# The first norm's sum of squares cut into two fp32r halves and summed by two products at blocks 38 and 39

## The chip, the cores and the metric

One NeuronCore of a Trainium2 chip runs the whole program. The metric is the device time of one execution in microseconds (us); lower is better. The engines named here: TensorE (PE, with its weight loads as PEld), VectorE (DVE), ScalarE (ACT), GpSimd (POOL) and SyncE (SP, which issues nearly all transfers).

## What is computed

One inference step of a two-layer decoder for 256 prompt tokens and 8 sample tokens that share all weights: 264 columns in all (`T = 264`), with a model width of 1024. Each layer is a mixer (layer 0: block-sparse attention beside a gated MLP; layer 1: stick-breaking attention beside a pooling mixer) and a feed-forward part with a short convolution. All parts begin with a root-mean-square norm. The part that the change touches is the very first norm and the projection behind it:

```python
def rmsnorm(x, g):
    xf = x.astype(jnp.float32)
    y = xf * lax.rsqrt(jnp.mean(xf * xf, axis=-1, keepdims=True) + EPS)
    return (y * g).astype(x.dtype)
...
    h = rmsnorm(x, norm_g)
    z = h @ w_in
    q, k, v, bu, bv = jnp.split(z, [...], axis=-1)
```

All arrays are float32.

## The kernel before

Activations lie transposed: the model width is on the 128 partitions in 8 tiles of 128x264, the tokens along the free axis. A matrix product is cut into blocks of 128x128 weights against one 128x264 tile. Each float32 operand is written as a high and a low part in the format fp32r (`wh`, `wl` for weights, `xg_h`, `xg_l` for activations), and each block is three products on TensorE: high by high, high by low, low by high. The layer-0 input projection has 20 output tiles of 8 blocks each, 160 blocks; one output tile of PSUM collects 8 blocks.

The high part of the weights is made by ScalarE (a copy that rounds), the low part by VectorE (the difference), for a weight tile of 8 blocks at a time: weight tile t holds blocks 8t to 8t+7. In the loop of blocks (`run`), `split(t)` makes the parts up to three tiles ahead, on lines L321. For the first tiles the order is written out by hand ahead of the loop: `part`, `operand`, `square` and `whole(tt)` (L734 for the high part, L735 for the low part). Four slots hold weight parts, so tile 7 takes the place of tile 3, which is free when block 31 is through. Tile 5 comes from a transfer of its own; tiles 6 and 7 come from one transfer of 1 MB, which is issued at 9.64 us.

The norm's factor R is needed only after the projection, since it scales columns. So the squares of the eight input tiles are made on ScalarE (`square`, L713), summed to one 128x264 tile by three additions on VectorE (`add`, L759), and summed over partitions by a product with a matrix of ones into the PSUM tile `ns_n0`. ScalarE turns that into R with a logarithm and an exponential (L502, L503). Then VectorE scales the output tiles that have collected by then (`in0_evac`, L807 for bv), which frees their PSUM banks, and makes the scaled rotary tables (L775). Blocks 0 to 31 are the output tiles bv0 to bv3 in four banks; blocks 32 to 39 (q0) and 40 to 47 (q1) go to two spare banks of another pool; block 48 needs the bank of bv0 again.

The program is traced in Python in the order of the code. A planner then puts each engine's instructions in order, by its own idea at build time of when each is ready: an instruction whose inputs come early may go ahead of one that was traced before it. `tc.keep_in_program_order(i)` pins an instruction behind the one that was traced just before it on the same engine. An engine issues its instructions strictly in the order so set, and waits where an input is missing. In this stage all instructions of TensorE are pinned (`fixed[0] = True`), and so are those of `whole`, `square`, `operand` and `add`; those of `split` are not. Hooks are functions called between blocks: `blk(38, f)` calls `f` after block 37 and ahead of block 38. `norm0` is hooked there in the kernel before: the float32 product, the logarithm and exponential, then the pinned evacuations.

Of the kernel before, what the change touches and what calls it, by code (L numbers as in the profile page):

```python
# [9 lines left out]
F32 = mybir.dt.float32  # L10
# [4 lines left out]
ALU = mybir.AluOpType  # L15
# [4 lines left out]
D = 1024  # L20
# [3 lines left out]
T = SEQ + NS  # L24
# [190 lines left out]
def tile_decoder_step(ctx: ExitStack, tc: tile.TileContext, a):  # L215
    nc = tc.nc
    v, s, g = nc.vector, nc.scalar, nc.gpsimd
# [14 lines left out]
    pe = TensorE()  # L232
# [10 lines left out]
    def f4(name, shape=(P, 4, T), dt=F32):  # L243
        return up.tile(list(shape), dt, tag="u", name=name)
# [7 lines left out]
    def at(name):  # L252
        return psa.tile([P, 512], F32, tag="at", name=name)
# [14 lines left out]
    def vec(n):  # L268
        o, w = _VEC[n]
        return VEC[:, o:o + w]  # L270
# [24 lines left out]
    def wtiles(tt):  # L295
        return [wsp.tile([P, 8 * P], F32R, tag=f"w{x}", name=f"w{x}{tt}") for x in "hl"]
# [97 lines left out]
    first, o = [], 0  # L394
# [34 lines left out]
    onesr = con.tile([P, P], F32R, name="onesr")  # L429
# [13 lines left out]
    class Norm:  # L443
# [8 lines left out]
        def add(self, m, src=None):  # L452
            q = sm.tile([P, T], F32, tag="sq", name=f"sq_{self.name}{m}")
            i = s.activation(q, X[:, m, :] if src is None else src, AF.Square)
            if src is not None:
                tc.keep_in_program_order(i)
            if m == KD - 1 and self.two:
                self.last.append(q)
            elif self.acc is None:
                self.acc = q  # L460
            elif m == (0 if self.seeded else 1):
                n = sm.tile([P, T], F32, tag="acc", name=f"acc_{self.name}", bufs=2)
                g.tensor_tensor(n, self.acc, q, ALU.add)
                self.acc = n
            else:
                g.tensor_tensor(self.acc, self.acc, q, ALU.add)

        def finish(self, pin=False, cut=False, inv=False):
            if not cut:
                return rstd_of([self.acc] + self.last, 1.0 / D, self.name, pin, eps=not self.seeded)  # L470
            return rstd_of(cut_sum(self.acc, self.name), 1.0 / D, self.name, pin, w=onesr, inv=inv)

    cast = [None]

    def cut_sum(x, name):
        if name in ("f0", "n1", "f1"):
            h, l = [pp.tile([P, 384], F32R, tag="p", name=f"acc{c}_{name}")[:, o:o + T] for c, o in (("h", 24), ("l", 16))]
        else:
            h, l = [sm.tile([P, T], F32R, tag="rz", name=f"acc{c}_{name}", bufs=4) for c in "hl"]
        cast[0] = s.activation(h, x, AF.Copy)  # L480
        g.tensor_tensor(l, x, h.bitcast(F32), ALU.subtract)
        return [h, l]

    def rstd_of(parts, scale, name, pin=False, bank=None, w=None, inv=False, eps=True):
        p = (bank or at)(f"ns_{name}")
        for i, x in enumerate(parts):
            mm = pe.matmul(p[:, :T], ones if w is None else w, x, start=i == 0, stop=i == len(parts) - 1)
            if pin:
                tc.keep_in_program_order(mm)
        R = sm.tile([P, T], F32, tag="R", name=f"R_{name}", bufs=2)  # L490
        if inv:
            L = sm.tile([P, T], F32, tag="rinv", name=f"L_{name}", bufs=1)
            s.activation(L, p[:, :T], AF.Ln, bias=epst, scale=scale)
            s.activation(R, L, AF.Exp, scale=-0.5)
            last[0] = s.activation(L, L, AF.Exp, scale=0.5)
            return R, L
        return rstd_from(p, scale, name, eps, R)

    def rstd_from(p, scale, name, eps=True, R=None):
        if R is None:  # L500
            R = sm.tile([P, T], F32, tag="R", name=f"R_{name}", bufs=2)
        s.activation(R, p[:, :T], AF.Ln, bias=epst if eps else 0.0, scale=scale)  # L502
        last[0] = s.activation(R, R, AF.Exp, scale=-0.5)  # L503
        return R
# [175 lines left out]
    def residual(gain, name, operand=True, R=None, plain=False):  # L680
        xg = [mv(f"xg_{name}{i}") for i in range(2)] if operand else None
        nrm = Norm(name, not operand)

        def evac(m, o):
            m = m[1]
            if R is not None and not plain:
                z = sm.tile([P, T], F32, tag="rz", name=f"z_{name}{m}", bufs=4)
                v.tensor_tensor(z, o, R, ALU.mult)
                o = z
            if plain and m == KD - 1:  # L690
                end(o)
                return
            v.tensor_tensor(X[:, m, :], X[:, m, :], o, ALU.add)
            if operand:
                operand_tile(xg[m // 4], m, X[:, m, :], gain[:, m:m + 1])
            nrm.add(m)
            if not operand:
                s.activation(X[:, m, :], X[:, m, :], AF.Copy, scale=gain[:, m:m + 1])
        return xg, nrm, evac
# [9 lines left out]
    nrm = Norm("n0")  # L709
    sqw = [f4(f"sqw{i}") for i in range(2)]  # L710
# [15 lines left out]
    def whole(tt, cut=(0, 8)):  # L726
        if tt not in splits:
            splits[tt] = wtiles(tt)
        c = slice(cut[0] * P, cut[1] * P)
        h, l = [x[:, c] for x in splits[tt]]  # L730
        ci = chunk_of[tt]
        o = (tt * 8 - coff[ci]) * P
        src = raws[ci][:, o + c.start:o + c.stop]
        tc.keep_in_program_order(s.activation(h, src, AF.Copy))  # L734
        tc.keep_in_program_order(v.tensor_tensor(l, src, h.bitcast(F32), ALU.subtract))  # L735
# [24 lines left out]
    add(sqw[0], sqw[0], sqw[1])  # L760
    add(sqw[0][:, 0:2, :], sqw[0][:, 0:2, :], sqw[0][:, 2:4, :])
    add(sqw[0][:, 0, :], sqw[0][:, 0, :], sqw[0][:, 1, :])
    whole(5)
    nrm.acc = sqw[0][:, 0, :]
    whole(6)
    rope = f4("rope")
    R0, held = [], []

    def norm0():
        R = nrm.finish(pin=True)  # L770
        R0.append(R)
        for m, o in held:
            tc.keep_in_program_order(in0_evac(m, o))
        for i in range(2):
            tc.keep_in_program_order(v.tensor_tensor(rope[:, i, :], CS[:, i, :], R, ALU.mult))  # L775

    maskb0 = con.tile([P, 384], BF16, name="maskb0")
    g.memset(maskb0[:, P:SEQ], 0.0)
# [9 lines left out]
    def in0_evac(m, o):  # L788
        n, t = m
        if not R0:  # L790
            held.append((m, o))
            return
        if n in "qk":
            d = (q4 if n == "q" else k4)[:, t, :]
            z = sm.tile([P, T], F32, tag="rz", name=f"rz_{n}{t}", bufs=4)
            v.stream_shuffle(z, o, shuf)
            if n == "q":
                v.scalar_tensor_tensor(d, o, SCALE, rope[:, 0, :], ALU.mult, ALU.mult)
            else:
                v.tensor_tensor(d, o, rope[:, 0, :], ALU.mult)  # L800
            if n == "q":
                v.scalar_tensor_tensor(z, z, SCALE, rope[:, 1, :], ALU.mult, ALU.mult)
            else:
                v.tensor_tensor(z, z, rope[:, 1, :], ALU.mult)
            v.tensor_tensor(d, d, z, ALU.add)
        else:
            return v.tensor_tensor({"v": v4, "bv": bv4, "bu": bu4}[n][:, t, :], o, R0[0], ALU.mult)  # L807
# [116 lines left out]
    def gm_mean():  # L924
        st0["acc"] = cut_sum(sum4(SUM1, bv4, "bsum"), "bsum")

    def gm_var():
        pmu = mmb("pmu")
        for i, x in enumerate(st0["acc"]):
            pe.matmul(pmu[:, :T], onesr, x, start=i == 0, stop=i == 1)  # L930
        mu = sm.tile([P, T], F32, tag="sq", name="mu")
        i = s.activation(mu, pmu[:, :T], AF.Copy, scale=1.0 / 512)
        behind(st0["exp", 5, 0], i)
        behind(st0["exp", 5, 1], i)
        ahead[18] = i, v.tensor_tensor(bv4, bv4, mu.unsqueeze(1).to_broadcast([P, 4, T]), ALU.subtract)
        sq4 = f4("sq4")
        s.activation(sq4, bv4, AF.Square)
        st0["acc"] = cut_sum(sum4(SUM2, sq4, "bsq"), "bsq")
# [36 lines left out]
    blk = lambda b, f, *x: hk.at(b / 8 - 1, f, *x)  # L975
# [12 lines left out]
        blk(92 + 6 * n, drip_of(vload, 2))  # L988
    for m in range(0, KD, 2):
        blk(120 + 4 * m, late_x, m)  # L990
    blk(38, norm0)
    blk(40, masks)
    blk(44, gm_first)
    blk(72, sm_q)
# [35 lines left out]
    xg, nrm, evac = residual(vec("f0"), "f0")  # L1030
    run(orders["out0"], pick([catA, catB]), evac, hk)
    fixed[0] = False
    R = nrm.finish(cut=True)
# [177 lines left out]
    blk = lambda b, f, *x: hk.at(b / 8 - 1, f, *x)  # L1211
# [31 lines left out]
    xg, nrm, evac = residual(vec("f1"), "f1")  # L1243
    run(orders["out1"], pick([catA, catB]), evac, hk)
    fixed[0] = False
    R, RI = nrm.finish(cut=True, inv=True)
    gelu_set()
    _, nrm, evac = residual(vec("fin"), "fin", operand=False, R=R, plain=True)
# [37 lines left out]
    o = P * KD * TF  # L1286
# [81 lines left out]
```

## Time and profile before

| what | value |
|---|---|
| median of 3 runs | 588.69 us (588.42 to 589.29) |
| the profiled execution's own time | 588.17 us |
| its span in the trace | 586.4 us |
| granted TensorE clock | 0.999 |
| PE busy | 579.3 us, 99% of the span |
| DVE busy | 433.4 us, 74% |
| ACT busy | 340.1 us, 58% |
| POOL busy | 47.7 us, 8% |

All times of instructions in this document are from the start of the span. A row of the timeline gives the start, the length, the engine, the source line, the operation, and output<-inputs by the program's names without their numbers (so `ns_n` is `ns_n0`, and `mm` any of the accumulating tiles); equal neighbours are merged with their count (x2), and what stands in brackets is how long the engine was idle before and what ended it. The ends of PE's rows are modelled, since matmuls overlap; its rate is read from the starts.

### The profile page before, as it was taken

How to read it: one execution, taken by the hardware profiler on the slowest of the kernel's cores; microseconds unless marked ns; L12 is line 12 of the kernel's file. 1: busy time of each engine (PE TensorE's matmuls, PEld its weight loads, DVE VectorE, ACT ScalarE, POOL GpSimd, SP SyncE). 2: the span in 40 equal slices, each digit the busy share in tenths (PEclk: the TensorE clock that was granted, in tenths of full speed). 3: DMA queues.
4: the chain of work that ended last, by engine and by line, in shares of the span. 5: the costliest groups of instructions: out<-in, count | busy, mean ns of one | idle time of the engine just before them, and what ended most of it. 6: DMA issues, size and time to landing. Idle time of an engine off the chain costs nothing.

```text
span 586.4 us, 12433 instructions
## 1 busy us (share of the span) xinstructions
PE 579.3 (99%) x4976; PEld 564.5 (96%) x4976; DVE 433.4 (74%) x778; ACT 340.1 (58%) x603; POOL 47.7 (8%) x62
## 2 busy tenths in 40 slices
PE   9999999999999999999999999999999999999995
PEld 8999979999999999999999879999999999999995
DVE  6999976787877878656669867777787777865561
ACT  7849746665655656544454557567565565664431
POOL 1001313200000000011030000120000000011011
PEclk9999999999999999999999999999999999999999
DMA  8999564554545455984557853555454546454502
GB/s 326 414 354 412 205 222 181 174 211 154 207 154 206 164 197 172 343 321 177 200 210 269 307 201 99 181 191 180 181 193 167 203 158 216 157 211 154 208 1 74
DMA packets 28140, 122.42 MB, mean 209 GB/s; under 512 B 3378, under 2 KB 5298, under 8 KB 16690
## 3 DMA queue, kind: packets, MB, share of 16 engines
q1 hardware_dynamic: 27792, 121.30, 57.6%
q8 instruction: 39, 0.64, 0.4%
q10 hardware_dynamic: 290, 0.32, 0.2%
q14 instruction: 19, 0.16, 0.1%
HBM read 117.65 MB, written 3.96 MB: 207 GB/s over the span
## 4 chain that ended last, share of the span: by engine, by line
PE 99%; DVE 0%; ACT 0%; DVEq 0%; issue 0%
PE mm L227 92%; PE sc L227 1%; PE pv_l L227 1%; PE pav L227 1%; PE warm L227 1%; PE pt L230 1%; PE Z L227 1%; PE S L227 1%; PE pf L227 0%; DVE yo L1294 0%; PE pm L227 0%; PE vtp_v L230 0%; PE ns_end L227 0%; PE ns_n L227 0%; PE po_l L230 0%; PE vtp_sgu L230 0%
## 5 line engine op out<-in xcount | busy, mean ns | idle before, releaser
L321 ACT ACTIVATE wh<-raw 128x1024 fp32r<-128x1024 f32 x177 | 187.5, 1060 | 195.2 <-PE mm L227 187.6
L321 DVE TENSOR_TENSOR wl<-raw,wh 128x1024 fp32r<-128x1024 f32 x177 | 216.9, 1226 | 107.9 <-ACT wh L321 106.9
L227 PE MATMUL mm<-xg_f_h,wh 128*128 128x264 f32 x704 | 199.9, 284 | 0.0
L227 PE MATMUL mm<-xg_f_h,wl 128*128 128x264 f32 x704 | 199.8, 284 | 0.0
L227 PE MATMUL mm<-xg_f_l,wh 128*128 128x264 f32 x704 | 198.6, 282 | 0.0
L227 PEld LDWEIGHTS mm<-xg_f_l,wh 128*128 128x128 f32 x704 | 132.8, 189 | 0.0
L227 PEld LDWEIGHTS mm<-xg_f_h,wh 128*128 128x128 f32 x704 | 132.5, 188 | 0.0
L227 PEld LDWEIGHTS mm<-xg_f_h,wl 128*128 128x128 f32 x704 | 132.4, 188 | 0.0
L227 PE MATMUL mm<-a_h,wh 128*128 128x264 f32 x352 | 100.0, 284 | 0.0
L227 PE MATMUL mm<-a_h,wl 128*128 128x264 f32 x352 | 99.9, 284 | 0.0
L227 PE MATMUL mm<-a_l,wh 128*128 128x264 f32 x352 | 99.3, 282 | 0.0
L227 PEld LDWEIGHTS mm<-a_l,wh 128*128 128x128 f32 x352 | 66.4, 189 | 0.0
L227 PEld LDWEIGHTS mm<-a_h,wh 128*128 128x128 f32 x352 | 66.2, 188 | 0.0
L227 PEld LDWEIGHTS mm<-a_h,wl 128*128 128x128 f32 x352 | 66.2, 188 | 0.0
L227 PE MATMUL mm<-xg_h,wh 128*128 128x264 f32 x160 | 42.9, 293 | 0.0
L227 PE MATMUL mm<-xg_h,wl 128*128 128x264 f32 x160 | 41.7, 284 | 0.0
L227 PE MATMUL mm<-xg_l,wh 128*128 128x264 f32 x160 | 41.5, 284 | 0.0
L227 PE MATMUL mm<-xg_n_h,wh 128*128 128x264 f32 x128 | 36.8, 287 | 0.0
L227 PE MATMUL mm<-xg_n_h,wl 128*128 128x264 f32 x128 | 36.3, 284 | 0.0
L227 PE MATMUL mm<-xg_n_l,wh 128*128 128x264 f32 x128 | 36.2, 283 | 0.0
L227 PEld LDWEIGHTS mm<-xg_h,wh 128*128 128x128 f32 x160 | 28.6, 189 | 1.8 <-issue 1.2
L227 PEld LDWEIGHTS mm<-xg_l,wh 128*128 128x128 f32 x160 | 28.6, 189 | 0.0
(264 smaller groups left out, 852.2 us busy)
## 6 DMA issues: line engine op xcount, KB each, us to landing
raw<-in_w SPq DMA_DIRECT2D x89, 1024.0 KB, 4.8
K<-in_kt SPq DMA_DIRECT2D x32, 256.0 KB, 5.4
V<-in_vp SPq DMA_DIRECT2D x32, 256.0 KB, 5.5
raw<-in_w SPq DMA_DIRECT2D x3, 512.0 KB, 7.1
xw<-in_xw SPq DMA_DIRECT2D x3, 388.0 KB, 4.8
X<-in_x SPq DMA_DIRECT2D x4, 264.0 KB, 5.7
out_y<-yo SPq DMA_DIRECT2D x3, 184.0 KB, 2.3
out_k<-k SPq DMA_DIRECT2D x1, 528.0 KB, 7.5
```

The source lines that it names most:

```text
L227: return self.keep(nc.tensor.matmul(*x, **k))
L230: return self.keep(nc.tensor.transpose(*x, **k))
L321: for i, j in zip((s.activation(h, src, AF.Copy), v.tensor_tensor(l, src, h.bitcast(F32), ALU.subtract)), ahead.pop(tt, ())):
```

## The change

The sum of squares is no longer multiplied as float32. `cut_sum` gets a form for it (`pin=True`): ScalarE copies the sum to a high half in fp32r, pinned where it is traced, between the last `square` and the high part of weight tile 5; VectorE makes the low half, pinned where it is traced, between the low parts of weight tiles 5 and 6. The product with ones becomes two fp32r products into `ns_n0`: the high half's ahead of block 38, the low half's ahead of block 39. The logarithm, the exponential and the evacuations move from the hook at 38 to the one at 39, behind the second product. The PSUM tile is claimed ahead of the loop and no longer at block 38.

```diff
-    def cut_sum(x, name):
+    def cut_sum(x, name, pin=False):
...
             h, l = [sm.tile([P, T], F32R, tag="rz", name=f"acc{c}_{name}", bufs=4) for c in "hl"]
         cast[0] = s.activation(h, x, AF.Copy)
+        if pin:
+            tc.keep_in_program_order(cast[0])
+            return [h, l], lambda: tc.keep_in_program_order(v.tensor_tensor(l, x, h.bitcast(F32), ALU.subtract))
         g.tensor_tensor(l, x, h.bitcast(F32), ALU.subtract)
         return [h, l]
...
     add(sqw[0][:, 0, :], sqw[0][:, 0, :], sqw[0][:, 1, :])
+    x0, low0 = cut_sum(sqw[0][:, 0, :], "n0", pin=True)
     whole(5)
-    nrm.acc = sqw[0][:, 0, :]
+    low0()
     whole(6)
...
     def norm0():
-        R = nrm.finish(pin=True)
+        p = at("ns_n0")
+
+        def one(i):
+            tc.keep_in_program_order(pe.matmul(p[:, :T], onesr, x0[i], start=i == 0, stop=i == 1))
+
+        blk(38, one, 0)
+        blk(39, one, 1)
+        blk(39, lambda: root0(p))
+
+    def root0(p):
+        R = rstd_from(p, 1.0 / D, "n0")
         R0.append(R)
-        for m, o in held:
+        for m, o in held[:4]:
             tc.keep_in_program_order(in0_evac(m, o))
         for i in range(2):
             tc.keep_in_program_order(v.tensor_tensor(rope[:, i, :], CS[:, i, :], R, ALU.mult))
+        for m, o in held[4:]:
+            in0_evac(m, o)
...
-    blk(38, norm0)
+    norm0()
```

## Prediction

> **What bounds the kernel now.** I read the page's table of engines first, then the chain of waits in order of time for the first 60 us, then the timeline of each engine from 12 to 24 us, where the change lies.
>
> ```profile
> PE 579.3 (99%) x4976; PEld 564.5 (96%) x4976; DVE 433.4 (74%) x778; ACT 340.1 (58%) x603; POOL 47.7 (8%) x62
> 4.78 14.14 PE mm L227 x114
> 18.92 0.45 PE ns_n L227 x2
> 19.36 21.15 PE mm L227 x174
> PEld mm L227 <- issue: 2.8, 6, 0.8
> ```
>
> TensorE is busy for 99% of the span, and the chain runs through it alone: 114 products (38 blocks), the sum for the norm, then 174 more. The last row, of the view of waits, is the largest stop ahead of ordinary weight loads: 2.8 us in the whole span. So a product saved on TensorE is time saved, and a wait put into TensorE's stream is time lost, for little downstream could give it back.
>
> ```profile
> 18.51 0.28 PE L227 MATMUL mm<-xg_l,wh 128*128 128x264 f32 x1
> 18.64 0.28 PE L227 MATMUL mm<-xg_h,wl 128*128 128x264 f32 x1
> 18.76 0.61 PE L227 MATMUL ns_n<-sqw,ones 128*128 128x264 f32 x2
> 19.01 0.48 PE L227 MATMUL mm<-xg_h,wh 128*128 128x264 f32 x1
> 19.32 0.28 PE L227 MATMUL mm<-xg_l,wh 128*128 128x264 f32 x1
> 19.44 0.28 PE L227 MATMUL mm<-xg_h,wl 128*128 128x264 f32 x1
> 19.57 0.29 PE L227 MATMUL mm<-xg_h,wh 128*128 128x264 f32 x1
> 22.74 0.28 PE L227 MATMUL mm<-xg_h,wl 128*128 128x264 f32 x1
> 22.86 0.34 PE L227 MATMUL mm<-xg_h,wh 128*128 128x264 f32 x1
> 23.04 0.28 PE L227 MATMUL mm<-xg_l,wh 128*128 128x264 f32 x1
> ```
>
> Ordinary products start every 0.12 us. The float32 sum comes at 18.76; block 38 really begins 0.12 before its second product, at 19.20, and block 39 at 19.57. So the sum costs 0.44 us (the chain says 0.45). At 22.86, block 48, one step is 0.18 instead of 0.12: the bank of bv0 comes free a touch late.
>
> ```profile
> 14.06 1.35 ACT L713 ACTIVATE sqw<-xw 128x264 f32<-128x264 f32 x4
> 15.32 1.05 ACT L734 ACTIVATE wh<-raw 128x1024 fp32r<-128x1024 f32 x1
> 18.61 1.06 ACT L734 ACTIVATE wh<-raw 128x1024 fp32r<-128x1024 f32 x1 [2.25 <-DMA raw<-in_w]
> 19.57 1.05 ACT L321 ACTIVATE wh<-raw 128x1024 fp32r<-128x1024 f32 x1
> 20.52 0.46 ACT L502 ACTIVATE R_n<-ns_n,epst 128x264 f32<-128x264 f32 x1
> 21.02 0.43 ACT L503 ACTIVATE R_n<-R_n 128x264 f32<-128x264 f32 x1
> 15.51 1.25 DVE L759 TENSOR_TENSOR sqw<-sqw,sqw 128x1056 f32<-128x1056 f32 x1
> 16.80 1.18 DVE L759 TENSOR_TENSOR sqw<-sqw 128x528 f32<-128x528 f32 x2
> 17.89 1.22 DVE L735 TENSOR_TENSOR wl<-raw,wh 128x1024 fp32r<-128x1024 f32 x1
> 19.70 1.23 DVE L735 TENSOR_TENSOR wl<-raw,wh 128x1024 fp32r<-128x1024 f32 x1 [0.59 <-ACT wh L734]
> 20.84 1.22 DVE L321 TENSOR_TENSOR wl<-raw,wh 128x1024 fp32r<-128x1024 f32 x1
> 21.99 0.46 DVE L796 STREAM_SHUFFLE rz_q<-mm 128x264 f32<-128x264 f32 x1
> 22.34 1.43 DVE L807 TENSOR_TENSOR bv<-mm,R_n 128x264 f32<-128x264 f32 x4
> ```
>
> This is the stretch that decides. On ScalarE the high part of weight tile 5 (15.32) goes ahead while VectorE still adds the squares; the additions end at 16.80 + 1.18 = 17.98. Then ScalarE waits for the transfer of tiles 6 and 7, which lands at 18.61. All this lay hidden: TensorE needs tile 5 only at block 40, 8 x 3 x 0.12 us ahead of block 48 (22.86), at about 19.93.
>
> **The change, part by part.** *TensorE.* Two fp32r products at 0.12 each replace 0.44: -0.20 us. By itself TensorE would reach the first at 18.76, block 38 at 18.88, the second at 19.24 and block 39 at 19.36.
>
> *ScalarE: the new cast of the high half.* It is pinned between the last square and tile 5. Its input is the third addition, so ScalarE, which issues in order, stands from 15.41 until 17.98, and what was done at 15.32 comes behind it: tile 5's high part, then tile 6's.
>
> *VectorE: the low half.* It is pinned behind tile 5's low part, which waits for tile 5's high part, which waits for the cast. And TensorE's second product waits for the low half ahead of block 39. So the wait is a chain: additions, cast, high 5, low 5, low half, product, and behind the product all of TensorE.
>
> ```profile
> 35.56 0.43 DVE L805 TENSOR_TENSOR q<-q,rz_q 128x264 f32<-128x264 f32 x1
> 36.08 0.27 ACT L977 ACTIVATE qz_l<-q 64x32 f32<-64x32 f32 x1 [0.40 <-DVE q L805]
> 4.06 0.52 ACT L437 ACTIVATE xg_h<-xw 128x264 fp32r<-128x264 f32 x1 [1.02 <-DMA xw<-in_xw]
> 4.63 0.65 PEld L227 LDWEIGHTS mm<-xg_h,wh 128*128 128x128 f32 x4 [0.33 <-ACT xg_h L437]
> ```
>
> Its links: a hand-over from VectorE to ScalarE takes 0.09 (35.99 to 36.08), one to TensorE 0.05 (taken from 4.58 to 4.63). ScalarE goes on 0.31 after starting a 128x264 tile (four squares: (1.35 - 0.41)/3) and 0.96 after a weight tile (18.61 to 19.57). VectorE starts a low part 1.09 after ScalarE starts the high part (18.61 to 19.70), goes on 1.14 later (19.70 to 20.84), and needs 0.43 for a 128x264 difference. The cast isn't in the trace; the square of the same shape bounds it below (0.41), the scaled copy above (0.52).
>
> *What the planner does with ScalarE's hole.* The high part of tile 7 (19.57, L321) isn't pinned. Its slot is free when block 31 is through: 18 + 1 products ahead of 18.76, about 16.6, well before the additions end. The trace shows that the planner fills such holes: the shuffle of q0 (21.99) was traced behind the four pinned bv evacuations (22.34) and runs ahead of them, because they wait for R. That this shuffle goes first also says that in the plan low 7 was through before R was, so the plan had tile 7 landed early. The chip has it land at 18.61. So I expect tile 7's high part in the hole ahead of the cast, where it holds the cast until the transfer lands. The two ends are then:
>
> - hole unfilled: cast 17.98 + 0.09 = 18.07, high 5 at 18.38, low 5 at 19.47, low half 20.61 to 21.04, product at 21.09. TensorE waits 21.09 - 19.24 = 1.85, block 39 begins at 21.21 instead of 19.57: +1.64.
> - hole filled by tile 7: high 7 at 18.61, cast 19.57, high 5 at 19.88, low 5 at 20.97, low half 22.11 to 22.54, product at 22.59. Block 39 begins at 22.71: +3.14. TensorE waits twice, at the first product (cast ready at 19.57 + 0.41 + 0.05 = 20.03, so 1.27) and at the second (20.52 to 22.59: 2.07).
>
> I take the second end, because tile 7 is ready some 1.4 us before the additions end, and keep both for the range.
>
> *Behind it.* Block 40 comes 0.36 after block 39 (23.07), with tile 5's low part ready since 22.2: no new wait. R comes at 22.59 + 0.28 + 0.05, then from 20.52 to 21.44 it takes 0.92: 23.84; bv0 is out by about 24.6, and block 48 comes at 26.0. So the 0.06 at 22.86 goes: -0.06. VectorE's queue after tiles 6 and 7 is some 1.7 us later than before and TensorE over 3, so later evacuations and low parts gain slack. The moved hook carries no transfer; SP's queue keeps its order, and the pool slot of the squares, held about 3 us longer, can delay one tile load at most as long as TensorE is late itself. GpSimd gets nothing. The earlier claim of the PSUM tile and `held[4:]` (empty, since q0 ends with block 39) cost nothing.
>
> *Sum:* 3.14 - 0.06 = +3.08 us, in which the -0.20 is contained. Against the profiled execution's 588.17 (span 586.4 and 1.8 around it) 591.25. That execution lies 0.52 under the median of 588.69, so for a median I say 588.69 + 3.08 = 591.8.
>
> **The rivals.** *Hole unfilled* (tile 7 stays behind tile 6, as in the order of before). For it: tracing order, and that the plan's transfer of tile 7 may be later than the additions. +1.64 - 0.06 = +1.58: 590.3.
>
> *The clock halves.*
>
> ```profile
> 0.78 4.00 PE L227 MATMUL warm<-const-bfloat16-1.0 128*128 128x256 bf16 x18 [0.78 <-PEq L1334]
> ```
>
> The first 18 products take 4.00/18 = 0.22 each, those after 4.63 only 0.12: TensorE starts at about half rate for some 3.6 us. If a wait of 2 us set it back, some 3.6 us at half rate would lose 1.8 more: 593.6. Against it: two separate waits, each shorter than that stretch; for it: the trace has no idle stretch of that size to show either way.
>
> The Trainium skill, "TensorE: Matmul & The Clock Gate", Part 1, says the clock drops to half after at least one idle window of about 3.4 us and comes back after as long a busy one. By that rule neither wait fills a window and nothing is added. No run here shows such a gap yet.
>
> *Not slower: tile 5 keeps its place ahead of the cast.* If ScalarE ran high 5 at 15.32 as now and only the cast waited, low 5 would stay at 17.89, the low half would follow at 19.03 (17.89 + 1.14) and end at 19.46, and the product start at 19.51: a wait of 0.27 against the 0.20 saved and the 0.06, zero in sum: 588.7. What decides is whether the high part of tile 5 starts before 18.0. Against it: the pin puts it behind the cast, and ScalarE's rows are in order throughout.
>
> **How the numbers follow.** A difference of 0.2% (1.18 us) is about what a measurement here can tell. Hole filled 0.48; hole unfilled 0.32; clock 0.06; tile 5 ahead 0.09; something else that the new plan does 0.05. Filled and clock are slower by over 0.2%, of unfilled (0.27%) I give 0.28 to slower and 0.04 to within; tile 5 ahead is within; of the rest 0.03 goes to faster and 0.02 to within. Slower 0.82, within 0.15, faster 0.03. The range holds both ends with 0.4 below the unfilled case (late waits that give a little back) and 0.6 above the filled one (a slower cast, a hand-over): 589.9 to 592.4, with 0.8 inside.
>
> **What would show it.** Right: on ScalarE an fp32r copy of the sum standing ahead of tile 5's high part (L734), with idle time before it; tile 7's high part (L321) ahead of both; a VectorE difference of 128x264 behind tile 5's low part, ending near 22.5; two `ns_n` products 2 to 2.6 us apart, with PE idle before them; no 0.18 step at block 48; 0.12 us steps throughout. Wrong: high 5 at 15.3; the two products 0.5 us apart with no idle; a step of 0.22 after the gap (clock); or a wait of similar size taken away elsewhere.

## The result, and the profile after

| what | before | after |
|---|---|---|
| median | 588.66 us (588.42 to 589.29, 6 runs) | 593.48 us (592.65 to 594.13, 6 runs) |
| profiled execution | 588.17 us | 593.34 us |

The change makes the kernel 4.8 us slower: ratio 1.0082, interval 1.0072 to 1.0092. The forecast of 591.8 had the direction; the time lies 1.1 above its range. Three stops of TensorE, not one, make most of the difference. First the page's table of engines, then three rows of the view of waits (us waited in all, times, longest), after; the last row is the kernel before, for the transposes:

```profile
PE 580.8 (98%) x4976; PEld 565.3 (96%) x4976; DVE 434.0 (73%) x779; ACT 343.4 (58%) x606; POOL 46.9 (8%) x62
PEld mm L227 <- DVE bv L823: 2.0, 1, 2.0
PEld ns_n L227 <- DVE accl_n L483: 1.8, 1, 1.8
PEld pt L230 <- DVE st L848: 0.6, 1, 0.6
...
PEld pt L230 <- DVE st L832: 0.2, 1, 0.2
```

ScalarE has three instructions more, though the change adds one to it. TensorE's longest single wait is not the one for the low half (`accl_n`) but one for `bv`, the evacuation that needs R. The third is at the first transposes of the attention (`pt`), where before the row had 0.2. The lines moved by up to 16: L737 and L738 are the parts that were L734 and L735, L505 and L506 the logarithm and exponential, L823 the evacuation.

TensorE's timeline after:

```profile
19.87 0.28 PE L227 MATMUL ns_n<-acch_n,onesr 128*128 128x264 f32 x1
20.24 0.28 PE L227 MATMUL mm<-xg_h,wl 128*128 128x264 f32 x1
22.15 0.39 PE L227 MATMUL ns_n<-accl_n,onesr 128*128 128x264 f32 x1 [1.63 <-DVE accl_n L483]
22.38 0.29 PE L227 MATMUL mm<-xg_h,wh 128*128 128x264 f32 x1
25.53 0.28 PE L227 MATMUL mm<-xg_h,wl 128*128 128x264 f32 x1
27.56 0.39 PE L227 MATMUL mm<-xg_h,wh 128*128 128x264 f32 x1 [1.74 <-DVE bv L823]
27.78 0.28 PE L227 MATMUL mm<-xg_l,wh 128*128 128x264 f32 x1
27.90 0.28 PE L227 MATMUL mm<-xg_h,wl 128*128 128x264 f32 x1
```

Read the starts, and compare them with the same products in the prediction's rows. The last product of block 38 is 0.80 later (19.44 to 20.24): this execution came to the sum about 1.12 later, and the cheaper first product gives back 0.32. Block 39 is 2.81 later (19.57 to 22.38), so the low half's product and its wait take 2.01. Block 48 is 4.70 later (22.86 to 27.56), so the second wait takes 1.89. The end is 5.17 later, with 0.47 from there on, most of it at the transposes: -0.32 + 1.12 + 2.01 + 1.89 + 0.47 = 5.17. The 1.12 is no part of the change. TensorE runs at half rate at the start; by the granted clock in the traces it has full rate from 4.88 in this execution of before and from 6.71 here, and 1.8 us at half rate lose 0.9. In the ten profiled executions of this document that moment lies anywhere between 3.47 and 6.76, late in a kernel with the old start (6.29, the hook alone) and early in one with the new start (3.47, tile 5 ahead of the cast). Without the 1.12 the change costs 4.05 in this execution, which is 592.7 from the median of before; the lowest of the six runs is 592.65.

Why the waits: ScalarE, then VectorE, after.

```profile
19.12 0.42 ACT L480 ACTIVATE acch_n<-sqw 128x264 fp32r<-128x264 f32 x1 [2.60 <-DVE sqw L762]
19.45 1.99 ACT L737 ACTIVATE wh<-raw 128x1024 fp32r<-128x1024 f32 x2
21.35 1.04 ACT L321 ACTIVATE wh<-raw 128x1024 fp32r<-128x1024 f32 x1
22.58 0.48 ACT L505 ACTIVATE R_n<-ns_n,epst 128x264 f32<-128x264 f32 x1 [0.19 <-PE ns_n L227]
22.96 1.05 ACT L321 ACTIVATE wh<-raw 128x1024 fp32r<-128x1024 f32 x1
24.03 1.28 ACT L625 ACT_TABLE_LOAD   x1
25.32 1.28 ACT L506 ACT_TABLE_LOAD   x1
26.61 0.42 ACT L506 ACTIVATE R_n<-R_n 128x264 f32<-128x264 f32 x1
28.40 1.28 ACT L937 ACT_TABLE_LOAD   x1
```

```profile
20.53 1.23 DVE L738 TENSOR_TENSOR wl<-raw,wh 128x1024 fp32r<-128x1024 f32 x1 [1.44 <-ACT wh L737]
21.67 0.42 DVE L483 TENSOR_TENSOR accl_n<-sqw,acch_n 128x264 fp32r<-128x264 f32 x1
27.07 1.45 DVE L823 TENSOR_TENSOR bv<-mm,R_n 128x264 f32<-128x264 f32 x4 [0.76 <-ACT R_n L506]
```

Top to bottom, ScalarE stands 2.60 us for the additions, casts (19.12), and only then makes the high parts of tiles 5 and 6 (19.45, x2) and 7 (21.35). VectorE's low part of tile 5 (20.53) and the low half (21.67) follow; the second product starts at 22.15. That is the predicted chain. Then comes what the prediction did not have: between the logarithm (22.58) and the exponential (26.61) stand the high part of another weight tile (tile 8) and two table loads. The first, L625, is `gelu_set`, a preload for later work; the second belongs to the exponential, whose table it displaced. The gelu's own line then loads its table again (L937, at 28.40), so ScalarE's three additional instructions are the cast and two loads. The exponential starts 4.03 behind the logarithm. The same two instructions in the trace of before:

```profile
21.75 1.04 ACT L321 ACTIVATE wh<-raw 128x1024 fp32r<-128x1024 f32 x1
22.81 1.28 ACT L622 ACT_TABLE_LOAD   x1
```

There they stand behind the exponential (21.02) and cost R nothing.

### The profile page after: what moved, and what is told of

It reads as the page before. It is cut to its first block, busy times and chain, and to the rows that moved or that the text cites. A ratio compares the mean times of both kernels' runs of the same rounds, so it can differ in the third digit from the quotient of the medians.

```text
span 591.5 us, 12440 instructions
## 1 busy us (share of the span) xinstructions
PE 580.8 (98%) x4976; PEld 565.3 (96%) x4976; DVE 434.0 (73%) x779; ACT 343.4 (58%) x606; POOL 46.9 (8%) x62
## 4 chain that ended last, share of the span: by engine, by line
PE 93%; DVE 2%; DMA 2%; ACT 1%; issue 1%; DVEq 0%; SPq 0%; ACTq 0%
PE mm L227 87%; DMA xw<-in_xw 2%; PE sc L227 1%; PE pv_l L227 1%; PE pav L227 1%; PE pt L230 1%; PE Z L227 1%; ACT wh L737 0%; DVE sqw L762 0%; DVE wl L321 0%; DVE p L848 0%; PE pf L227 0%; DVE yo L1310 0%; PE pm L227 0%; ACT xg_h L437 0%
```

## The experiments

Each experiment was run beside the kernel before, so the medians of before differ a little (588.35 and 588.61). The theory from these traces: two causes that don't depend on each other, the cast ahead of tile 5 (low half's wait) and the root moved to hook 39 (split of logarithm and exponential), with the transposes as a consequence. The rival: the low half's wait is the only cause, and the rest follows from everything being late.

**The hook alone.** The kernel before, its float32 product and all else kept, with the norm one block later:

```diff
-    blk(38, norm0)
+    blk(39, norm0)
```

> The kernel before with one number changed: the hook of the first norm at 39 and no longer at 38; the float32 product stays. Two-waits theory: the hook alone brings the high part of tile 8 and the table load between the logarithm and the exponential, R is late by some 3.5 us, block 48 waits about 2.6 us: 591.3 us. Rival, one wait only: without the halves nothing is late, 588.7 within 0.4.

Measured: 593.39 us (592.13 to 595.16, 4 runs) against 588.35; ratio 1.0084, interval 1.006 to 1.0109. By the medians the hook alone costs as much as the whole change, 2.1 more than the 591.3 expected. ScalarE and TensorE of this kernel:

```profile
20.52 0.48 ACT L502 ACTIVATE R_n<-ns_n,epst 128x264 f32<-128x264 f32 x1
21.57 1.06 ACT L321 ACTIVATE wh<-raw 128x1024 fp32r<-128x1024 f32 x1 [0.57 <-DMA raw<-in_w]
22.65 1.28 ACT L622 ACT_TABLE_LOAD   x1
23.94 1.28 ACT L503 ACT_TABLE_LOAD   x1
25.24 0.42 ACT L503 ACTIVATE R_n<-R_n 128x264 f32<-128x264 f32 x1
...
23.47 0.28 PE L227 MATMUL mm<-xg_h,wl 128*128 128x264 f32 x1
26.18 0.39 PE L227 MATMUL mm<-xg_h,wh 128*128 128x264 f32 x1 [2.42 <-DVE bv L807]
27.20 0.42 PE L227 MATMUL mm<-xg_h,wh 128*128 128x264 f32 x1
```

The logarithm starts at 20.52 exactly as before, and the exponential at 25.24 in place of 21.02: 4.22 later, made of the wait for tile 8's transfer, its high part and both loads. Block 48 comes 2.71 behind the product ahead of it. No cut sum is needed for this; the rival falls. That the total equals that of the whole change is chance: the wait for the low half is missing here. The last row is one of a stretch in which each product takes 0.22, from about 26.8 to 30.1, which costs some 1.5 us; the lowest of the four runs is 592.13. The transposes' stop of 0.6 stands in this trace too, so it doesn't need the low half.

**The pair pinned behind the exponential.** The kernel after, with one order edge: `ahead[t]` names what the parts of weight tile t must follow, and the gelu preload is pinned behind tile 8's high part.

```diff
         R0.append(R)
+        ahead[8] = (last[0],)
```

> The changed kernel, with the high part of weight tile 8 put behind the exponential that makes R, so that the table load for the gelu cannot come between the logarithm and the exponential. Two-waits theory: the changed kernel loses time at two places, at the low half's product (+1.7 us, the queue behind the cast) and at block 48 (+1.9 us, R late by two table loads), and a smaller one (0.45) in the scores at block 96 that follows from the second. Then block 48's wait goes and the one at the product stays: 593.5 - 1.9 - 0.45 = 591.1 us, at most 591.6. Rival, one wait only: block 48 is late because the low half is late, whatever the tables do; then R's bank stays late and the time stays within 0.5 us of 593.5.

Measured: 590.3 us (590.13 to 591.26, 7 runs); ratio 1.0032, interval 1.002 to 1.0043. Of 4.8 us 1.95 are left; the time is 0.8 under the expected 591.1. ScalarE:

```profile
22.05 0.48 ACT L505 ACTIVATE R_n<-ns_n,epst 128x264 f32<-128x264 f32 x1 [0.20 <-PE ns_n L227]
22.57 0.42 ACT L506 ACTIVATE R_n<-R_n 128x264 f32<-128x264 f32 x1
23.30 1.05 ACT L321 ACTIVATE wh<-raw 128x1024 fp32r<-128x1024 f32 x1
24.36 1.28 ACT L625 ACT_TABLE_LOAD   x1
```

Exponential 0.52 behind the logarithm, one table load, and no wait at block 48; the low half's wait of 1.8 stands as in after, so the rival falls. The edit gives 2.9, more than the 1.89 of the stop; part of the rest may be the half rate that can follow a stop (below), but these runs don't say how much. The transposes' stop is 0.8 here although R is on time, so it isn't a consequence of the late R, as the theory had it.

**Tile 5 ahead of the cast.** The kernel after with `whole(5)` traced first. This was the prediction's rival on the other side, made to happen:

```diff
-    x0, low0 = cut_sum(sqw[0][:, 0, :], "n0", pin=True)
     whole(5)
+    x0, low0 = cut_sum(sqw[0][:, 0, :], "n0", pin=True)
     low0()
```

> The changed kernel with the cast of the sum traced behind the high part of weight tile 5, and nothing else. Two-waits theory: the wait at the low half's product shrinks from 1.9 to about 0.3 us, but the exponential still stands behind two table loads, R comes at about 25.0 and block 48, due at 22.9, waits some 2.6 us: 588.7 + 0.1 + 2.6 = 591.4 us. Rival, one wait only: with the low half early block 48 is on time too, and the time is that of the kernel before, 588.7 within 0.5.

Measured: 593.28 us (591.51 to 593.56, 4 runs); ratio 1.0082, interval 1.0065 to 1.0099. By the median hardly anything is gained (593.48 to 593.28), although the wait for the low half is nearly gone (0.2). Tile 5's high part now starts at 15.13, ahead of the cast. ScalarE and TensorE of the profiled execution, the 591.51:

```profile
17.83 0.43 ACT L480 ACTIVATE acch_n<-sqw 128x264 fp32r<-128x264 f32 x1 [1.65 <-DVE sqw L762]
...
22.71 0.28 PE L227 MATMUL mm<-xg_h,wl 128*128 128x264 f32 x1
25.75 0.39 PE L227 MATMUL mm<-xg_h,wh 128*128 128x264 f32 x1 [2.76 <-DVE bv L823]
```

TensorE reaches block 48 earlier and meets a late R again, so it waits 3.04 there. The two waits cover each other in part: block 48 starts 7.05 behind the high half's product here and 6.80 in a second profile, against 7.69 and 6.99 in the two profiles of after, some 0.4 earlier on average. Behind this wait products come every 0.12, and this run has the 591.4 that was expected; the other three (593.25 to 593.56) lie about 2 above. Their granted clock is 0.995 to 0.996 against 0.998 here, which would fit a half-rate stretch, but runs of before at 0.996 are no slower, so this isn't shown. Like with like, the edit may therefore gain more than the medians say.

**Both mended.** The two edits above in one kernel, `whole(5)` first and the edge on `ahead[8]`:

```diff
+    whole(5)
     x0, low0 = cut_sum(sqw[0][:, 0, :], "n0", pin=True)
-    whole(5)
...
+        ahead[8] = (last[0],)
```

> Both edits: the cast behind tile 5's high part, and tile 8's high part behind the exponential. Two-waits theory: the product with the low half waits about 0.3 us, block 48 not over 0.1, 0.20 is saved by the fp32r products: 588.7 us within 0.4, the same as before. Rival: the two halves cost something elsewhere (the start of the kernel, the start of TensorE's clock, memory) that the changed kernel shows in its first 9 us (1.1 us later than the kernel before): then 589.8 us.

Measured: 589.22 us (588.84 to 589.77, 10 runs); ratio 1.0013, interval 1.0003 to 1.0022. Both waits are gone, and 0.87 us are left, 0.5 more than the theory and 0.6 less than the rival expected. VectorE and TensorE of this kernel, then of before:

```profile
48.27 1.22 DVE L321 TENSOR_TENSOR wl<-raw,wh 128x1024 fp32r<-128x1024 f32 x1
49.67 0.42 DVE L849 CUSTOM_DVE_ANT_0 p<-S,maskb 128x256 f32<-128x256 f32 x1
...
49.16 0.22 PE L230 MATMUL pt<-CST,p 64*128 64x64 f32 x1
50.15 0.58 PE L230 MATMUL pt<-CST,p 64*128 64x64 f32 x11 [0.77 <-DVE st L849]
```

```profile
48.38 0.42 DVE L832 CUSTOM_DVE_ANT_0 p<-S,maskb 128x256 f32<-128x256 f32 x1
48.92 1.22 DVE L321 TENSOR_TENSOR wl<-raw,wh 128x1024 fp32r<-128x1024 f32 x1
...
48.78 0.67 PE L230 MATMUL pt<-CST,p 64*128 64x64 f32 x12
```

Before, the reduction of attention scores (L832) goes first and the low part of weight tile 16 after it. Now the low part goes first, the reduction (L849) starts 1.29 later, and the transposes stop for 0.99 from start to start (49.16 to 50.15), where before all twelve take 0.67. The plan of VectorE's order has changed 28 us away from the edit; which of the edits' parts changed it there is not shown.

**The score reduction first.** The same, with tile 16's low part behind the reduction of head 3:

```diff
-            v.tensor_tensor_reduce(out=pr[:, c], ...)
+            j = v.tensor_tensor_reduce(out=pr[:, c], ...)
+        if h == 3:
+            ahead[16] = st0["exp", 1, 1], j
```

> The kernel with both edits (cast behind tile 5's high part, tile 8's high part behind the exponential) and a third: the low part of weight tile 16 goes behind the reduction of the scores of head 3 on VectorE. Theory of the planner's order: the 0.85 us that the kernel with both edits still waits ahead of the first transposes (block 112) is the low part of tile 16 taken ahead of that reduction, which frees the PSUM bank. Then the wait shrinks to 0.2 or less and the time is 589.2 - 0.7 = 588.5 us, level with before (588.35). Rival, VectorE is full: the added 0.43 us of the low half in a stretch where VectorE never idles is paid whatever the order; then the wait moves to another place and the time stays within 0.3 of 589.2.

Measured: 588.64 us (588.32 to 589.11, 11 runs) against 588.61; ratio 1.0002, interval 0.9992 to 1.0011. The rival falls. So does that of the run with both edits: this execution comes to the sum about as late (19.40 and 19.47) and its kernel is level all the same, so the start wasn't the cost. The view of waits:

```profile
PEld ns_n L227 <- DVE accl_n L483: 0.3, 1, 0.3
PEld pt L230 <- DVE st L849: 0.2, 1, 0.2
```

All that the change cost is accounted for, in this order of mending: from +4.8 to +1.95 by R's chain, to +0.87 by the low half's wait, to level by the reduction's place. What remains of the change, two cheap products with a last wait of 0.3, is worth nothing that can be measured.

**The low half one block later.** The last wait taken away too:

```diff
-        blk(39, one, 1)
-        blk(39, lambda: root0(p))
+        blk(40, one, 1)
+        blk(40, lambda: root0(p))
```

> The same three edits, and the low half's product and the root moved from the hook at 39 to the one at 40. The low half is ready about 0.25 us after TensorE would take it at 39 and before it would at 40, and the logarithm is held by tile 7's high part either way. Theory: the wait of 0.26 us at the product goes, nothing else moves: 588.2 us, 0.1 to 0.2 under before, hardly more than can be measured. Rival: R comes later and block 48 waits for it, 0.4 or more: 588.7 us or over.

Measured: 588.32 us (587.92 to 588.92, 11 runs) against 588.61; ratio 0.9997, interval 0.9988 to 1.0006. That is the change with every cost that was found removed; no wait at block 48 is found either, so the rival falls. It isn't told apart from the kernel before: its median is 0.3 lower, and by the rows its products save 0.20.

```profile
20.11 0.28 PE L227 MATMUL ns_n<-accl_n,onesr 128*128 128x264 f32 x1
20.23 0.28 PE L227 MATMUL mm<-xg_h,wh 128*128 128x264 f32 x1
```

One fp32r product takes 0.12, as forecast.

**The clock.** The half-rate stretch of the hook-alone run asked whether after has it too. The kernel after, profiled a second time:

> The changed kernel again, unaltered, for a second look at its start and at TensorE's rate behind the waits. The waits found so far (1.7, 1.9, 0.45) sum to 4.0 us of the 4.8 measured. Theory of the clock: the rest is TensorE at half rate, at the start or behind a wait, by chance from one execution to the next; this execution then starts its first blocks at another time than the first look did (4.68 with steps of 0.22 to 6.6), or shows steps of 0.22 behind the waits at 20 or 25 us. Rival, the start belongs to the change: the first blocks look as in the first look.

Measured: 594.01 us, one run. TensorE:

```profile
24.66 0.28 PE L227 MATMUL mm<-xg_h,wl 128*128 128x264 f32 x1
26.69 0.39 PE L227 MATMUL mm<-xg_h,wh 128*128 128x264 f32 x1 [1.74 <-DVE bv L823]
27.32 0.42 PE L227 MATMUL mm<-xg_l,wh 128*128 128x264 f32 x1
27.54 0.42 PE L227 MATMUL mm<-xg_h,wl 128*128 128x264 f32 x1
...
30.76 0.28 PE L227 MATMUL mm<-xg_h,wl 128*128 128x264 f32 x1
```

The wait at block 48 is 2.03, the same as in the first profile. Yet here the products behind it, from 27.32 to 30.6, take 0.22 each, 15 of them: 15 x 0.10 = 1.5 us lost. In the first profile they keep 0.12. The low half's product waits 1.22 from start to start here against 1.91 there. So the two executions reach nearly the same time (593.34 and 594.01) by different shares. The start did not show the difference that the theory asked for: the first products run at 0.22 to about 6.7 in both profiles. That the start nevertheless doesn't belong to the change is said above, from the other kernels.

The kernel with tile 5 first, profiled a second time:

> The kernel with only the cast moved behind tile 5's high part, again and unaltered: its wait of 3.04 us at block 48 was followed by full rate in the first look (591.5 us), while three further executions took 593.3 to 593.6. Theory of the clock: after a wait of this length TensorE may run its next 12 to 15 products at 0.22 instead of 0.12, which costs 1.2 to 1.5 us, in some executions and not in others; at about 593.3 us the trace shows that stretch, at 591.5 it doesn't. Rival: the 1.8 us between executions lie elsewhere, with steps of 0.12 throughout.

Measured: 591.93 us, one run.

```profile
23.50 0.28 PE L227 MATMUL mm<-xg_h,wl 128*128 128x264 f32 x1
26.17 0.39 PE L227 MATMUL mm<-xg_h,wh 128*128 128x264 f32 x1 [2.39 <-DVE bv L823]
```

A wait of 2.67, and full rate behind it. For a time near 591.5 the theory expects that, so the execution agrees with it; a trace of 593.3, where the stretch should show, is not among the runs. Whether a wait is followed by half rate isn't set by its length alone: 2.03 and 2.71 were once each, 2.03, 2.67 and 3.04 were not.

The granted clock in the traces shows more. It drops to 0.50 from 27.24 to 30.65 in the second profile of after and from 26.77 to 30.18 with the hook alone, 3.41 us both times. Both drops come 20.48 us behind the moment at which the start's half rate ended (6.76 and 6.29), which is six times 3.41, and the full-rate stretches of the other eight executions, 580.27 and 583.68 long, are 170 and 171 times it. So the clock seems to be set at instants 3.41 apart, whose place differs from execution to execution. In these two executions TensorE's recorded idle time (1.74 and 2.42) lies whole between two such instants. In the first profile of after an instant (27.19) cuts the same 1.74 into 1.37 and 0.37, and in the two profiles with tile 5 first the largest piece is 1.80 and 1.63; the low half's wait of 1.63 in after lies whole between two instants and isn't followed by half rate. The place of a wait between these instants thus goes far to tell the cases apart; but 1.80 without half rate beside 1.74 with it says that the idle time is not the exact measure, and no run moved a wait to test this.

## Why the prediction was right in direction and short in size

- *TensorE saves 0.20.* Right: 0.12 a product.
- *The low half's wait is a chain through the cast and tile 5.* Right link by link. Its length for an unfilled hole, 1.85, stands beside 1.79 in the first profile of after (1.91 less one step) and 1.10 in the second, where ScalarE's chain ran 0.87 earlier than in the first (its cast at 18.25 against 19.12) and TensorE only 0.17.
- *Tile 7 fills ScalarE's hole.* Wrong: the rows have cast, 5 and 6, then 7. The shuffle of q0 going ahead of the evacuations was no proof that the planner saw tile 7 early. The end taken, 3.14, was the wrong one of the two; the other, 1.64, happened. In the first profile block 39 is 1.69 later, the 1.12 of the start set apart. With R's chain whole that case measured 590.3, which is also what the prediction gave it, but not for its reasons alone: it is 1.95 above its own before where the prediction had 1.58, and the transposes' wait, of 0.8 there, was not in its sum.
- *R takes 0.92 from logarithm to R, so block 48 has no wait.* **This step failed**, and with it the account of the size. The 0.92 was read from two rows of before that are neighbours on ScalarE, and was taken over for the new order. The exponential now starts 4.03 behind the logarithm in place of 0.50, with tile 8's high part and two table loads between. The sum gained 1.89 at block 48 where it had -0.06. The moved hook was weighed for SP's queue, GpSimd, slots and the PSUM tile, but not for what ScalarE's own order would admit.
- *The sum.* Term by term it had 3.14 for block 39, -0.06 for block 48 and nothing for the transposes; the first profile has 1.69, 1.89 and 0.47, together 4.05. The first two errors, -1.45 and +1.95, largely cancel, so it is luck that the forecast came within 1.7 of the median. The median is 4.82 above before; the 0.8 beyond 4.05 is of the size of the clock's share, which differs by run (0.9 at the start, 1.5 behind a wait) and was not split further.
- *The clock's rival* had a chance of 0.06 for a wait of 2 us being followed by 1.8 lost. It happens in part of the executions, with 1.5. (The opening half rate from which the 3.6 us were read lasts until 4.88 by the granted clock, and the first products after 4.63 start 0.17 apart, not 0.12.) The Trainium skill, "TensorE: Matmul & The Clock Gate", Part 1, asks for an idle window of about 3.4 us; waits of 2.03 and 2.71 were enough here at times, so the measurement decides against the rule as the prediction used it. The same part calls the window free-running; the drops 20.48 us, six times 3.41, behind the start's change of rate agree with that, and the mixed outcomes fit a dependence on where the wait falls in it.
- *Later evacuations and low parts gain slack.* Wrong at one place: tile 16's low part went ahead of the reduction, for most of 0.47 in after and for 0.87 once all else was mended.
- *Tile 5 ahead: 588.7.* Right for the mechanism it described, once R's chain and the reduction are put back: 588.64. As a single edit it measured 593.28.

That the later hook lets tile 8 between logarithm and exponential is shown by the hook alone; why the planner does so at 39 and not at 38 is only argued. Tile 8 takes tile 4's slot, and block 39 is the last to read it. At 39 the logarithm's place in the plan is one block nearer to that moment, so tile 8 may be ready in the plan while the exponential still is not. No run varied the slot.

## What to carry to other kernels

When a step moves, even by one block, ask of each engine that runs two dependent instructions of it what else could be ready between them. A preload without inputs can go anywhere that its pin allows, and a table load inside a logarithm-exponential pair puts two loads into the pair, not one; an edge that puts the preload behind the pair is one line. A cast in an in-order queue holds all that is behind it for its input, so trace first what doesn't need the sum. And undo causes together as well as one at a time: here two waits covered each other in part, and mending only the one that had been foreseen showed almost no gain in the median.

## What the runs showed of the hardware

- The two table loads take 1.28 us each and stand back to back with the activations around them (24.03, 25.32, 26.61): 2.58 for the pair. The Trainium skill, "ScalarE: Activation LUTs", "What ACT_TABLE_LOAD costs", gives about 1283 ns for the load, which agrees, and a further 1380 ns of drain for each switch, which these rows don't show.
- A stop of 2 to 3 us on TensorE can bring 3.41 us at half rate behind it (granted clock 0.50), in some executions and not in others of the same kernel, with 1.5 us at stake each time. In both such traces it began 20.48 us, six times 3.41, behind the end of the half rate at the start.
- The half rate at the start ended between 3.47 and 6.76 us of the span in the ten profiled executions, whatever the kernel. With the hook at 38, the sum's first product came at 18.70 to 19.87.
